# Sums of weight blocks made in DRAM by adding DMAs in place of VectorE additions

## The chip, the cores and the metric

The kernel runs on one core of a Trainium2 chip. The core has TensorE (PE; PEld is its weight load), VectorE (DVE), ScalarE (ACT) and GpSimd (POOL). DMAs are started from the queues of SyncE (SP), ACT and POOL and moved by 16 DMA engines. The metric is device time of one execution in microseconds, the median of several runs; a profile is of one execution.

## What is computed

The reference is a trunk of two layers on 512 tokens of width 1024, all in float32. Both layers widen to 2048.

```python
h = x                                               # (1, 512, 1024)
# layer 0: pooling mixer
u = rms_norm(h) @ pool_w_in                         # 1024 -> 4096
v, gate = split(u, 2)
p = multiscale_pool(v)                              # 4 groups of 512, windows 2, 4, 8, 16
m = einsum('btgc,gcd->btgd', p, w_grp) * scale
h = h + (m * silu(gate)) @ pool_w_out               # 2048 -> 1024
# layer 1: HGRN2, 16 heads of 128, chunks
q, fz, i, gate = split(rms_norm(h) @ hgrn_w_in, 4)  # 1024 -> 8192
o = hgrn2_chunk_scan(q, k(fz), i, cumsum(log_f(fz)))
h = h + (rms_norm_heads(o) * silu(gate)) @ hgrn_w_out
return rms_norm(h)
```

## The kernel before

**Products.** Each product of float32 operands is made of three matmuls of halves: an operand x is cut into hi (x rounded, made by ScalarE at L97) and lo (x minus hi, made by VectorE at L98), and `mm3` (L128 to L131) adds hi·hi, hi·lo and lo·hi in PSUM. Weights come in blocks of 128 x 2 x 512 floats, 512 KB, into the tiles wraw (three buffers), and are cut into whi and wlo (six buffers each); `piece` (L100) does one block: a load on SP's queue, then the cut. PE works through such products nearly all the time.

**Layer 0.** `l0` starts with eight blocks of x (h) and eight half blocks of w0i, 256 KB each, then four loads of x in the other layout (xt, 512 KB) for the norm. The norm factor rn_l is made of the sums ss in two steps: VectorE computes ms (L253), POOL takes the power (L255). PE spreads it over the partitions by L197 (`spread`), ScalarE copies the spread factor to rb (L203), and rb is used by every later step of the layer. In PE's instruction list L197 stands before the seventh of the eight steps of the first gates' projection. Then four groups g follow: `values`, `pool`, `project_out` of the group before, `gates0`, `mixed`.

**Layer 1.** The groups run through `group`: values of the group (`inputs`), attention, gates, output projection of the group before. The values of the last two groups are made together by `inputs2` (L457), when g is 2. It multiplies a 2 x 2 block matrix (two halves of the tokens, two groups) with seven block products in place of eight. Four of the seven use sums of weight blocks. With W(row, col) a quarter of 512 x 512 floats, two wraw blocks, they are

- W5 = W(0,0) + W(0,1), then W6 = W5 + W(1,1), then W4 = W6 + W(1,0): one chain, kept in the tiles named chain;
- W7 = W(0,1) + W(1,1), made in place in wraw.

Each sum is made on VectorE by `add` (L477 to L480, the instruction is L479), from blocks loaded by `load` (L474), and then cut like any other weight block. The other operand of four products is a sum of token blocks, which layer 1 has written to DRAM earlier (sums_fac) and reads back by `again` (tiles s, L454).

**What sets the order.** The program is written with tiles; a scheduler orders the instructions of each engine by priority, dependences and free buffers when the kernel is built, and `tc.high_priority(AHEAD)` moves loads and cuts ahead. At run time each engine takes its list strictly in order, and an instruction that waits for a semaphore holds up what stands behind it. POOL has no DMAs in this kernel.

Of the kernel before, what the change touches and what calls it, by code (L numbers as in the profile page):

```python
# [32 lines left out]
F32 = mybir.dt.float32  # L33
# [22 lines left out]
AHEAD0 = 85  # L56
AHEAD = 300
FLOOR = 1e-26
LEVELS = (1, 2, 4, 8, 16, 32, 64)


# [5 lines left out]
def trunk(ctx: ExitStack, tc: tile.TileContext, xT, x_d, par, ident_d, causal_d, mask_d, fg_d, w0_in, w0_grp, w0_out, w1_in, w1_out, out):  # L67
# [155 lines left out]
            nc.vector.tensor_tensor(out=h[n], in0=acc, in1=h[n], op=ALU.add)  # L223


    with tc.tile_pool(name="l0", bufs=1) as l0:
        xs, pieces = [], []
        wv = w0_in.rearrange("(k p) n -> p k n", p=P)
# [34 lines left out]
        def values(g):  # L263
            vs = []
            wv = None if g == 0 else load_in(w0_in, g * GC)
            for n in range(GT):
                acc = accs[n] if g == 0 else project(wv, n, xs)
                v = l0.tile([P, 16 + T], F32, name="v", tag="v", bufs=4)
                nc.gpsimd.memset(v[:, 0:16], 0.0)
                nc.vector.tensor_tensor(out=v[:, 16:], in0=acc, in1=rb, op=ALU.mult)  # L270
                vs.append(v)
            return vs

        def pool(g, vs):
            w, out = WINDOWS[g], []
            for n in range(GT):
                cur, step = vs[n], 1
                while step < w:
                    nxt = l0.tile([P, 16 + T], F32, name="win", tag="win", bufs=2)
                    if 2 * step < w:  # L280
                        nc.gpsimd.memset(nxt[:, 0:16], 0.0)
                    nc.vector.tensor_tensor(out=nxt[:, 16:], in0=cur[:, 16:], in1=cur[:, 16 - step:16 + T - step], op=ALU.add)
                    cur, step = nxt, 2 * step
                nc.vector.tensor_tensor(out=cur[:, 16:16 + w], in0=cur[:, 16:16 + w], in1=pp[:, cnts[g]:cnts[g] + w], op=ALU.mult)
                p = small.tile([P, T], F32, name="p", tag="hg", bufs=2)
                nc.vector.scalar_tensor_tensor(out=p, in0=cur[:, 16:], scalar=1.0 / w, in1=vs[n][:, 16:], op0=ALU.mult, op1=ALU.subtract)
                out.append(halves(p, "p", 4, l0))
            return out

        def gates0(g):  # L290
            wg = wg0 if g == 0 else load_in(w0_in, DI + g * GC)
            out = []
            for n in range(GT):
                acc = gates[n] if g == 0 and n < 2 else project(wg, n, xs)
                gt = l0.tile([P, T], F32, name="gt", tag="gt", bufs=2)
                nc.vector.tensor_tensor(out=gt, in0=acc, in1=rb, op=ALU.mult)
                sg = l0.tile([P, T], F32, name="sg", tag="sg", bufs=2)
                nc.scalar.activation(out=sg, in_=gt, func=AF.Sigmoid)  # L298
                gs = l0.tile([P, T], F32, name="gs", tag="gs", bufs=4)
                nc.gpsimd.tensor_tensor(out=gs, in0=gt, in1=sg, op=ALU.mult)  # L300
                out.append(gs)
            return out

        def mixed(g, ps_, gates):
            wm = load_in(w0_grp[g])
            out = []
            for n in range(GT):
                acc = project(wm, n, ps_)
                z = small.tile([P, T], F32, name="z", tag="hg", bufs=2)
                c = C_PS + g * GT + n  # L310
                nc.vector.scalar_tensor_tensor(out=z, in0=acc, scalar=pp[:, c:c + 1], in1=gates[n], op0=ALU.mult, op1=ALU.mult)
                out.append(halves(z, "z", 8, l0))
            return out

        zprev = None
        for g in range(NG):
            vs = values(g)
            px = pool(g, vs)
            if zprev is not None and g < NG - 1:
                project_out(load_out(w0_out, g - 1), zprev)  # L320
            gts = gates0(g)
            z = mixed(g, px, gts)
            if g == NG - 1:
                project_out(load_out(w0_out, g - 1), zprev)
            zprev = z
# [24 lines left out]
    def hgrn(ctx, general, h):  # L350
# [107 lines left out]
        def inputs2(g):  # L458

            w = w1_in.rearrange("(k p) n -> p k n", p=P)

            def block(row, col, i):
                c = 2 * DI + (g + col) * GC
                return w[:, 4 * row + 2 * i:4 * row + 2 * i + 2, c:c + GC]

            def load(*a):
                raw = wpool.tile([P, 2, GC], F32, name="wraw", tag="wraw", bufs=RAW)
                with tc.high_priority(AHEAD):
                    nc.sync.dma_start(out=raw, in_=block(*a))  # L474
                return raw

            def add(out, x, y):  # L477
                with tc.high_priority(AHEAD):
                    nc.vector.tensor_tensor(out=out, in0=x, in1=y, op=ALU.add)  # L479
                return out  # L480

            def cut(x):
                hi = wpool.tile([P, 2, GC], F32R, name="whi", tag="whi", bufs=WB)
                lo = wpool.tile([P, 2, GC], F32R, name="wlo", tag="wlo", bufs=WB)
                with tc.high_priority(AHEAD):
                    split(x, hi, lo)
                return [(hi[:, 0], lo[:, 0]), (hi[:, 1], lo[:, 1])]

            def product(accs, x, pieces):
                for b, acc in enumerate(accs):  # L490
                    t = slice(b * P, (b + 1) * P)
                    for k, ((xh, xl), (wh, wl)) in enumerate(zip(x, pieces)):
                        mm3(acc, xh[:, t], xl[:, t], wh, wl, k == 0, k == 3)

            two = lambda: [ps.tile([P, T], F32, name="mm", tag="mm", bufs=4) for _ in range(2)]
            v = l1.tile([P, TB, GC], F32, name="vn", tag="vn", bufs=1)
            v1 = [l1.tile([P, GC], F32, name="v1", tag="gs", bufs=4) for _ in range(TB)]
            chain = []
            s = again

            def plus(out, acc, x):
                nc.vector.tensor_tensor(out=out, in0=acc, in1=x, op=ALU.add)  # L502

            def times(x, by, t):
                nc.scalar.activation(out=x, in_=x, func=AF.Copy, scale=by[:, t:t + 1])

            a = two()
            product(a, own[0], cut(load(0, 0, 0)) + cut(load(0, 0, 1)))
            for b in range(2):
                nc.scalar.copy(out=v[:, 2 + b], in_=a[b])  # L510
            a = two()
            product(a, own[1], cut(load(1, 0, 0)) + cut(load(1, 0, 1)))
            for b in range(2):
                plus(v[:, b], a[b], v[:, 2 + b])
                times(v[:, b], rn, b)
            pieces = []
            for i in range(2):
                x, y = load(0, 0, i), load(0, 1, i)
                chain.append(l1.tile([P, 2, GC], F32, name="chain", tag="f", bufs=2))
                pieces += cut(add(chain[i], x, y))  # L520
            c = two()
            product(c, s(0), pieces)
            s2 = s(1)
            pieces = [x for i in range(2) for x in cut(add(chain[i], chain[i], load(1, 1, i)))]
            a = two()
            product(a, s2, pieces)
            s3 = s(2)
            for b in range(2):
                plus(v1[b], a[b], v[:, 2 + b])
            pieces = []  # L530
            for i in range(2):
                x, y = load(0, 1, i), load(1, 1, i)
                pieces += cut(add(x, x, y))
            a = two()
            product(a, s3, pieces)
            s4 = s(3)
            for b in range(2):
                plus(v[:, 2 + b], a[b], v1[b])
                plus(v1[2 + b], c[b], v[:, 2 + b])
                plus(v1[b], c[b], v1[b])  # L540
                times(v1[2 + b], nrn, 2 + b)
                nc.scalar.dma_start(out=v_d[2 + b], in_=v1[2 + b])
            pieces = [x for i in range(2) for x in cut(add(chain[i], chain[i], load(1, 0, i)))]
            a = two()
            product(a, own[3], pieces)
            for b in range(2):
                plus(v[:, 2 + b], a[b], v[:, 2 + b])
                times(v[:, 2 + b], rn, 2 + b)
            a = two()
            product(a, s4, cut(load(1, 1, 0)) + cut(load(1, 1, 1)))  # L550
            for b in range(2):
                plus(v1[b], a[b], v1[b])
                times(v1[b], nrn, b)
                nc.scalar.dma_start(out=v_d[b], in_=v1[b])
            return v
# [411 lines left out]
```

## Time and profile before

| | us |
|---|---|
| median of 3 runs (lowest to highest) | 840.53 (840.23 to 841.55) |
| the profiled execution | 840.38 |
| its span, first to last instruction | 838.6 |
| PE busy in the span | 816.0 |
| VectorE busy | 582.5 |
| ScalarE busy | 295.1 |
| POOL busy | 151.4 |

The profiled execution takes 1.8 us more than its span. Busy time of PE is the union of its matmuls, which overlap: a matmul of 512 columns is listed with 0.39 us, but one starts every 0.23 us. The rows below are from this execution; "idle before" names what ended the idle time of an engine.

### The profile page before, as it was taken

To read this page: it belongs to the slowest core of one execution; us is meant where nothing else is said; L and a number is where in the kernel's file an instruction comes from. 1 tells how busy PE (TensorE), PEld (TensorE's weight loads), DVE (VectorE), ACT (ScalarE), POOL (GpSimd) and SP (SyncE) were. 2 spreads that over 40 slices of the span, in tenths; PEclk is the share of its full clock that TensorE was granted. 3 is DMA by queue.
4 is the path that set the end of the run, shared out by engine and by line. 5 is a ranking of instruction groups with operands and counts; after the bars stand their busy time and mean duration, and the time that the engine had idled before them with its cause. 6 is when DMAs were issued, how large, how long until landed. Compare 5 with 4: busy or idle time off the path is not lost.

```text
span 838.6 us, 10334 instructions
## 1 busy us (share of the span) xinstructions
PE 816.0 (97%) x3878; PEld 682.0 (81%) x3878; DVE 582.5 (69%) x889; ACT 295.1 (35%) x500; POOL 151.4 (18%) x198
## 2 busy tenths in 40 slices
PE   9999999999999999998999999999988999998995
PEld 8888888888888888887888788888767888887984
DVE  5787546844777463997489973279988545995764
ACT  7542133323235153415442242332236134223222
POOL 0020010002011041440134300305300031332200
PEclk9999999999999999999999999999999999999999
DMA  9532234323134155034733231233387243321202
GB/s 347 185 102 75 77 100 151 101 78 117 57 101 130 62 175 163 26 101 152 250 101 100 93 110 36 66 101 100 101 269 259 74 152 101 101 75 55 73 1 104
DMA packets 48299, 96.89 MB, mean 116 GB/s; under 512 B 3696, under 2 KB 8048, under 8 KB 48240
## 3 DMA queue, kind: packets, MB, share of 16 engines
q1 hardware_dynamic: 42336, 85.99, 31.4%
q10 hardware_dynamic: 5904, 10.15, 3.3%
q8 instruction: 32, 0.52, 0.2%
q14 instruction: 27, 0.22, 0.1%
HBM read 86.69 MB, written 9.44 MB: 115 GB/s over the span
## 4 chain that ended last, share of the span: by engine, by line
PE 76%; DVE 16%; DMA 3%; issue 2%; ACT 2%; POOL 0%; POOLq 0%; DVEq 0%; ACTq 0%
PE mm L130 23%; PE mm L129 23%; PE mm L131 22%; DVE r L720 4%; DVE wlo L98 4%; DMA wraw<-in_w1i 3%; PE a L775 2%; PE a L777 1%; PE a L753 1%; ACT whi L97 1%; DVE f L705 1%; DVE q L724 1%; DVE f L706 1%; PE a L736 1%; DMA wraw<-in_w1o 1%
## 5 line engine op out<-in xcount | busy, mean ns | idle before, releaser
L129 PE MATMUL mm<-xh,whi 128*128 128x512 f32 x624 | 244.3, 391 | 0.0
L131 PE MATMUL mm<-xh,wlo 128*128 128x512 f32 x624 | 243.0, 390 | 0.0
L130 PE MATMUL mm<-xl,whi 128*128 128x512 f32 x624 | 243.0, 389 | 0.0
L97 ACT CAST whi<-wraw 128x1024 fp32r<-128x1024 f32 (+1 forms) x140 | 141.5, 1025 | 226.5 <-PE mm L130 108.3
L98 DVE TENSOR_TENSOR wlo<-wraw,whi 128x1024 fp32r<-128x1024 f32 (+1 forms) x140 | 172.7, 1258 | 49.7 <-ACT whi L97 47.9
L131 PEld LDWEIGHTS mm<-xh,wlo 128*128 128x128 f32 x624 | 117.1, 188 | 24.7 <-DVE wlo L98 0.2
L129 PEld LDWEIGHTS mm<-xh,whi 128*128 128x128 f32 x624 | 117.2, 188 | 24.2 <-DVE h L223 0.3
L130 PEld LDWEIGHTS mm<-xl,whi 128*128 128x128 f32 x624 | 117.2, 188 | 23.8
L720 DVE RECIPROCAL r<-r 128x512 f32<-128x512 f32 x16 | 53.4, 3338 | 0.0
L131 PE MATMUL mm<-zh,wlo 128*128 128x512 f32 x128 | 49.8, 389 | 0.0
L129 PE MATMUL mm<-zh,whi 128*128 128x512 f32 x128 | 49.8, 389 | 0.0
L130 PE MATMUL mm<-zl,whi 128*128 128x512 f32 x128 | 49.8, 389 | 0.0
L223 DVE TENSOR_TENSOR h<-mm,h 128x512 f32<-128x512 f32 x32 | 21.9, 688 | 28.5 <-PE mm L131 28.1
L380 DVE TENSOR_TENSOR ht<-mm,ht 128x512 f32<-128x512 f32 x32 | 22.0, 687 | 27.9 <-PE mm L131 27.9
L129 PE MATMUL mm<-whi,z1h 128*128 128x512 f32 x96 | 37.9, 395 | 0.0
L300 POOL TENSOR_TENSOR gs<-gt,sg 128x512 f32<-128x512 f32 x16 | 21.9, 1372 | 87.9 <-ACT sg L298 87.9
L131 PE MATMUL mm<-whi,z1l 128*128 128x512 f32 x96 | 37.4, 390 | 0.0
L582 POOL TENSOR_TENSOR gs<-fz,s 128x512 f32<-128x512 f32 x16 | 22.4, 1402 | 83.3 <-ACT s L580 83.2
L130 PE MATMUL mm<-wlo,z1h 128*128 128x512 f32 x96 | 37.4, 389 | 0.0
L594 POOL TENSOR_TENSOR ro<-mo,mhalf 128x4 f32<-128x4 f32 x16 | 16.2, 1014 | 113.1 <-DVE mo L592 113.1
L130 PE MATMUL mm<-wlo,xh 128*128 128x512 f32 x88 | 34.6, 393 | 1.0 <-DVE wlo L98 1.0
L129 PE MATMUL mm<-whi,xh 128*128 128x512 f32 x88 | 34.7, 394 | 0.7 <-DVE v L502 0.7
(179 smaller groups left out, 1271.1 us busy)
## 6 DMA issues: line engine op xcount, KB each, us to landing
wraw<-in_w1i SPq DMA_DIRECT2D x74, 512.0 KB, 4.0
wraw<-in_w0i SPq DMA_DIRECT2D x28, 512.0 KB, 4.5
wraw<-in_w0o SPq DMA_DIRECT2D x16, 512.0 KB, 4.1
wraw<-in_w1o SPq DMA_DIRECT2D x16, 512.0 KB, 4.1
wraw<-in_w0g SPq DMA_DIRECT2D x8, 512.0 KB, 3.8
s<-sums_fac SPq DMA_DIRECT2D x16, 256.0 KB, 4.4
h<-in_xT SPq DMA_DIRECT2D x8, 256.0 KB, 5.3
wraw<-in_w0i SPq DMA_DIRECT2D x8, 256.0 KB, 5.3
```

The costliest lines, as they stand in the source:

```text
L97: nc.scalar.copy(out=hi, in_=src)
L98: nc.vector.tensor_tensor(out=lo, in0=src, in1=hi, op=ALU.subtract)
L129: nc.tensor.matmul(out, lh, rh, start=start, stop=False)
L130: nc.tensor.matmul(out, lh, rl, start=False, stop=False)
L131: nc.tensor.matmul(out, ll, rh, start=False, stop=stop)
L223: nc.vector.tensor_tensor(out=h[n], in0=acc, in1=h[n], op=ALU.add)
L300: nc.gpsimd.tensor_tensor(out=gs, in0=gt, in1=sg, op=ALU.mult)
L380: nc.vector.tensor_tensor(out=ht[b][:, c], in0=acc, in1=ht[b][:, c], op=ALU.add)
L582: nc.gpsimd.tensor_tensor(out=gs, in0=gt, in1=sg, op=ALU.mult)
L594: nc.gpsimd.tensor_tensor(out=ro[:, :, 0], in0=mo, in1=mhalf[:, :TB], op=ALU.pow)
L720: nc.vector.reciprocal(out=r, in_=r)
L775: nc.tensor.matmul(o[:, b], Ads[pr][:, j, t], v[:, b, n * P:(n + 1) * P], start=True, stop=b == 0)
```

## The change

The four sums of the third group are made in DRAM. A DRAM tensor wsum holds W5, W6, W7 and W4. A new function `weight_sums(step)` is called twice in each of groups 1, 2 and 3 of layer 0, in six steps: copy W(0,0) and W(0,1), add W(0,1) and W(1,1) to them, copy W5 to W6, add W(1,1), copy W6 to W4, add W(1,0). Each step is done in halves of 256 rows (512 KB), so there are 16 DMAs on POOL's queue, eight copies and eight with `accum_op=ALU.add`. `inputs2` then loads each sum as two blocks by `piece`, and `load`, `add`, `cut` and the tiles chain are gone from it. The setting dynamic_dma_scratch_size of the build goes from 512 to 1024.

```diff
+PAIRS = (2,)
+    wsum = {g: dram.tile([4, 4 * P, GC], F32, name=f"wsum{g}") for g in PAIRS}
+
+    def quarter(g, row, col):
+        c = 2 * DI + (g + col) * GC
+        return w1_in[row * 4 * P:(row + 1) * 4 * P, c:c + GC]
+
+    def weight_sums(step):
+
+        for g in PAIRS:
+            w5, w6, w7, w4 = (wsum[g][i] for i in range(4))
+            todo = (((w5, quarter(g, 0, 0), False), (w7, quarter(g, 0, 1), False)),
+                    ((w5, quarter(g, 0, 1), True), (w7, quarter(g, 1, 1), True)),
+                    ((w6, w5, False),), ((w6, quarter(g, 1, 1), True),),
+                    ((w4, w6, False),), ((w4, quarter(g, 1, 0), True),))[step]
+            for out_, in_, adding in todo:
+                for r in range(0, 4 * P, 2 * P):
+                    if adding:
+                        nc.gpsimd.dma_start(out=out_[r:r + 2 * P], in_=in_[r:r + 2 * P], accum_op=ALU.add)
+                    else:
+                        nc.gpsimd.dma_start(out=out_[r:r + 2 * P], in_=in_[r:r + 2 * P])
...
             vs = values(g)
+            if g:
+                weight_sums(2 * g - 2)
             px = pool(g, vs)
...
             gts = gates0(g)
+            if g:
+                weight_sums(2 * g - 1)
             z = mixed(g, px, gts)
...
-            pieces = []
-            for i in range(2):
-                x, y = load(0, 0, i), load(0, 1, i)
-                chain.append(l1.tile([P, 2, GC], F32, name="chain", tag="f", bufs=2))
-                pieces += cut(add(chain[i], x, y))
             c = two()
-            product(c, s(0), pieces)
+            product(c, s(0), pieces(wsum[g][0]))
             s2 = s(1)
-            pieces = [x for i in range(2) for x in cut(add(chain[i], chain[i], load(1, 1, i)))]
             a = two()
-            product(a, s2, pieces)
+            product(a, s2, pieces(wsum[g][1]))
...
-    nc = bacc.Bacc("TRN2", target_bir_lowering=False, num_devices=1, dynamic_dma_scratch_size=512)
+    nc = bacc.Bacc("TRN2", target_bir_lowering=False, num_devices=1, dynamic_dma_scratch_size=1024)
```

How the instruction lists change is shown at three places. First POOL at the start of layer 0, before:

```order
L94 MEMSET mhalf 128x8
L269 MEMSET v 128x16 x4
L255 ISA
L255 TENSOR_TENSOR rn_l_327<-ms,mhalf 128x4
L269 MEMSET v 128x16 x2
```

and now, each row with the semaphores that it waits for (DMASW0 to DMASW7 are counted up by POOL's own DMAs; the digits are their lanes):

```order
L292 MEMSET v 128x16 x4
L246 DMA wsum_104<-in_w1i 256x512 x4
L244 DMA wsum_104<-in_w1i 256x512 [waits DMASW0_49]
...
L244 DMA wsum_104<-in_w1i 256x512 [waits DMASW3_49]
L246 DMA wsum_104<-wsum_104 16x8192 [waits DMASW4_49]
...
L244 DMA wsum_104<-in_w1i 256x512 [waits DMASW1_49]
L246 DMA wsum_104<-wsum_104 16x8192 [waits DMASW2_49]
...
L244 DMA wsum_104<-in_w1i 256x512 [waits DMASW7_49,DMASW5_49]
L278 ISA
L278 TENSOR_TENSOR rn_l_328<-ms,mhalf 128x4 [waits DVE_49,Pool_49]
```

All 16 DMAs stand between the four memsets and rn_l (L246 are the copies, L244 the adds; L278 is what was L255), not in groups 1 to 3; 12 of them wait for an earlier one. PE's list is the same there.

Second VectorE at the beginning of `inputs2`, before (L608 and z1l belong to the gating of the group before, L72x to the preparation of this one):

```order
L720 RECIPROCAL r<-r 128x512
L479 TENSOR_TENSOR chain<-wraw 128x1024
L724 TENSOR_TENSOR q<-q,r 128x4x64
L725 TENSOR_TENSOR q<-q,f 128x4x64
L608 SCALAR_TENSOR_TENSOR z_4914<-a,pp,gs 128x512
L98 TENSOR_TENSOR wlo<-chain,whi 128x1024
L98 TENSOR_TENSOR z1l<-z_4914,z1h 128x512
L608 SCALAR_TENSOR_TENSOR z_4925<-a,pp,gs 128x512
L479 TENSOR_TENSOR chain<-wraw 128x1024
```

and now:

```order
L718 RECIPROCAL r<-r 128x512
L99 TENSOR_TENSOR wlo<-wraw,whi 128x1024 x3
L722 TENSOR_TENSOR q<-q,r 128x4x64
L723 TENSOR_TENSOR q<-q,f 128x4x64
L606 SCALAR_TENSOR_TENSOR z_4931<-a,pp,gs 128x512
L606 SCALAR_TENSOR_TENSOR z_4942<-a,pp,gs 128x512
L511 TENSOR_TENSOR vn<-mm,vn 128x512
```

Cuts of three blocks stand where one addition stood, ahead of the rest of the preparation.

Third SP's queue in `inputs2` and just behind it, before (L474 are its weight loads, L454 the loads of s, w1o the output weights):

```order
L106 DMA wraw<-in_w1i 128x2x512 x12
L474 DMA wraw<-in_w1i 128x2x512 x13
L454 DMA s<-sums_fac 128x2x256 x3
L474 DMA wraw<-in_w1i 128x2x512
L454 DMA s<-sums_fac 128x2x256 x2
L474 DMA wraw<-in_w1i 128x2x512 x2
L454 DMA s<-sums_fac 128x2x256
L474 DMA wraw<-in_w1i 128x2x512 x2
L106 DMA wraw<-in_w1o 128x1024
L454 DMA s<-sums_fac 128x2x256 x2
L106 DMA wraw<-in_w1o 128x1024 x3
```

and now:

```order
L107 DMA wraw<-in_w1i 128x2x512 x16
L107 DMA wraw<-wsum_104 128x2x512 x8
L481 DMA s<-sums_fac 128x2x256
L107 DMA wraw<-in_w1i 128x2x512
L481 DMA s<-sums_fac 128x2x256
L107 DMA wraw<-in_w1i 128x2x512
L107 DMA wraw<-in_w1o 128x1024
L481 DMA s<-sums_fac 128x2x256 x2
L107 DMA wraw<-in_w1o 128x1024 x2
L481 DMA s<-sums_fac 128x2x256 x4
L107 DMA wraw<-in_w1o 128x1024
```

The last 18 loads of weights for `inputs2` become 14, and the second eight loads of s stand behind all eight of wsum.

## Rows read from the trace of the kernel before

**Rows 1.** The page, part 1: busy us, share of span, instructions.

```profile
PE 816.0 (97%) x3878; PEld 682.0 (81%) x3878; DVE 582.5 (69%) x889; ACT 295.1 (35%) x500; POOL 151.4 (18%) x198
```

**Rows 2.** Stretches in the stage of `inputs2`: the first row names the columns.

```profile
core 0: us, PE busy (x) PEld busy (x) DVE busy (x) ACT busy (x) POOL busy (x), PEclk, DMA share, GB/s
600.00:660.00 60.00, 52.84 (x257) 42.67 (x256) 51.86 (x76) 24.82 (x30) 1.74 (x3) 1.00 0.72 234
...
620.00:630.00 10.00, 8.85 (x52) 7.36 (x50) 7.29 (x8) 3.42 (x4) 0.00 (x0) 1.00 0.91 298
```

**Rows 3.** Line L479: duration ns min/median/max, first and last start; then who waited.

```profile
L479 DVE TENSOR_TENSOR chain<-chain,wraw x4: 1208/1222/1227, 609.0 to 627.7; 128x1024 f32<-128x1024 f32 x4
L479 DVE TENSOR_TENSOR chain<-wraw x2: 1153/1178/1204, 601.9 to 607.3; 128x1024 f32<-128x1024 f32 x2
L479 DVE TENSOR_TENSOR wraw<-wraw x2: 1215/1220/1225, 616.5 to 622.5; 128x1024 f32<-128x1024 f32 x2
...
ACT whi L97: 15.2, 8
```

**Rows 4.** Chain of waits in `inputs2`: start us, us, what.

```profile
607.25 1.22 DVE chain L479
...
608.49 3.94 DMA wraw<-in_w1i
...
612.51 1.23 DVE chain L479
```

**Rows 5.** Waits from 553 to 700 us: waiter, releaser, us, times, longest.

```profile
PE mm L129 <- ACT whi L97: 2.8, 2, 1.6
...
PE mm L130 <- DVE wlo L98: 1.6, 2, 1.4
...
PE a L753 <- DVE Ad L739: 1.0, 1, 1.0
```

**Rows 6.** POOL in order of time at the start: start us, us, instruction.

```profile
0.90 0.24 POOL L269 MEMSET v<- 128x16 f32 x4
21.70 1.01 POOL L255 TENSOR_TENSOR rn_l<-ms,mhalf 128x4 f32<-128x4 f32 x1 [20.56 <-DVE ms L253]
```

**Rows 7.** PE in order of time, the spreading of the norm factor.

```profile
31.51 1.05 PE L197 MATMUL a<-ident,rn_l 128*128 128x128 f32 x8
```

**Rows 8.** Stretches of the first 30 us; columns as in rows 2.

```profile
0.00:5.00 5.00, 4.02 (x19) 4.03 (x20) 0.26 (x1) 2.42 (x4) 0.61 (x10) 1.00 0.63 199
5.00:10.00 5.00, 5.00 (x23) 3.96 (x23) 3.86 (x6) 3.79 (x7) 0.00 (x0) 1.00 1.02 368
10.00:15.00 5.00, 5.00 (x24) 4.14 (x23) 4.99 (x9) 4.79 (x8) 0.00 (x0) 1.00 1.04 391
15.00:20.00 5.00, 5.00 (x24) 4.14 (x23) 1.75 (x3) 4.25 (x8) 0.00 (x0) 1.00 1.02 414
20.00:25.00 5.00, 5.00 (x24) 4.14 (x23) 1.40 (x2) 3.27 (x5) 1.01 (x1) 1.00 0.64 233
25.00:30.00 5.00, 5.00 (x24) 4.14 (x23) 3.67 (x3) 2.16 (x3) 0.00 (x0) 1.00 0.72 233
```

**Rows 9.** DMA issues: line, queue, count, KB each, median us to landing.

```profile
wraw<-in_w1i SPq DMA_DIRECT2D x74, 512.0 KB, 4.0
wraw<-in_w0i SPq DMA_DIRECT2D x28, 512.0 KB, 4.5
...
h<-in_xT SPq DMA_DIRECT2D x8, 256.0 KB, 5.3
wraw<-in_w0i SPq DMA_DIRECT2D x8, 256.0 KB, 5.3
xt<-in_x SPq DMA_DIRECT2D x4, 512.0 KB, 6.7
```

**Rows 10.** Chain that ended last, PE's first pieces: start us, us, what.

```profile
0.98 4.64 PE a L86 x20
...
31.67 0.89 PE a L197 x8
```

More of the change, by code (lines that the diff above doesn't have):

```diff
@@ L458, in inputs2, with pieces, product @@
         def inputs2(g):
[L465 to L479, printed above, removed]
-                return out
[L482 to L489, printed above, removed]
+            def pieces(src):
+                v = src.rearrange("(k p) n -> p k n", p=P)
+                out = []
+                for i in range(0, 4, 2):
+                    hi, lo = piece(v[:, i:i + 2])
+                    out += [(hi[:, 0], lo[:, 0]), (hi[:, 1], lo[:, 1])]
+                return out
+            def product(accs, x, w):
                 for b, acc in enumerate(accs):
                     t = slice(b * P, (b + 1) * P)
-                    for k, ((xh, xl), (wh, wl)) in enumerate(zip(x, pieces)):
+                    for k, ((xh, xl), (wh, wl)) in enumerate(zip(x, w)):
                         mm3(acc, xh[:, t], xl[:, t], wh, wl, k == 0, k == 3)
@@ L497, in inputs2 @@
             v1 = [l1.tile([P, GC], F32, name="v1", tag="gs", bufs=4) for _ in range(TB)]
-            chain = []
             s = again
@@ L507, in inputs2 @@
             a = two()
-            product(a, own[0], cut(load(0, 0, 0)) + cut(load(0, 0, 1)))
+            product(a, own[0], pieces(quarter(g, 0, 0)))
             for b in range(2):
@@ L511, in inputs2 @@
             a = two()
-            product(a, own[1], cut(load(1, 0, 0)) + cut(load(1, 0, 1)))
+            product(a, own[1], pieces(quarter(g, 1, 0)))
             for b in range(2):
@@ L529, in inputs2 @@
                 plus(v1[b], a[b], v[:, 2 + b])
[L530 to L533, printed above, removed]
             a = two()
-            product(a, s3, pieces)
+            product(a, s3, pieces(wsum[g][2]))
             s4 = s(3)
@@ L542, in inputs2 @@
                 nc.scalar.dma_start(out=v_d[2 + b], in_=v1[2 + b])
-            pieces = [x for i in range(2) for x in cut(add(chain[i], chain[i], load(1, 0, i)))]
             a = two()
-            product(a, own[3], pieces)
+            product(a, own[3], pieces(wsum[g][3]))
             for b in range(2):
@@ L549, in inputs2 @@
             a = two()
-            product(a, s4, cut(load(1, 1, 0)) + cut(load(1, 1, 1)))
+            product(a, s4, pieces(quarter(g, 1, 1)))
             for b in range(2):
```

## The prediction

> **What bounds the kernel now.** First the page: PE is busy for 816.0 us of the span of 838.6 [rows 1]. So the time is PE's work plus the 22.6 us in which PE stands, and an edit to another engine or to a queue counts only where it makes PE stand or lets it go on. Two places matter, and the code names them: the stage that the change relieves (`inputs2`, layer 1, third group) and the start, where the order of the change puts its new DMAs.
>
> The stretches by stage come next [rows 2]. From 600 to 660 us PE is busy for 52.84 us of 60: it stands for 7.16 us, a third of all that it loses in the kernel. The DMA engines are at 0.91 there between 620 and 630. The lines of that stage say why [rows 3]: eight VectorE additions at L479, 1.18 to 1.22 us each, sum the weight blocks, and ScalarE, which cuts the result, waited 15.2 us for them. The chain of waits [rows 4] shows the pattern: a load of wraw, then an addition, then the next load. The waits of PE [rows 5] that come from there are 2.8 us on ScalarE's whi and 1.6 us on VectorE's wlo; 1.0 us on the causal copy (Ad) has another cause.
>
> The start is read last. POOL clears four borders by 1.14 us, does nothing for 20.56 us, and computes the norm factor rn_l at 21.70 us, in 1.01 us [rows 6]. PE uses it in L197 at 31.51 us [rows 7], so rn_l has about 8.8 us to spare. L197 stands in the middle of a projection, and PE takes its instructions in order: whatever delays rn_l past 31.5 us stops PE. In the same stretch the DMA engines are full, 1.02 to 1.04 of their time at 368 to 414 GB/s from 5 to 20 us [rows 8].
>
> **The change part by part.** Removed from layer 1: the eight additions (2 x 1.178 + 4 x 1.222 + 2 x 1.220 = 9.7 us of VectorE) and four of 18 weight loads, 0.52 MB each, since a sum is now read as one block. VectorE's order there becomes plain cuts. I take back the 7.16 us that PE stands less what waits for something else (the 1.0 us above and about as much on ScalarE's kt and other pieces, some 1.7 us): 5.5 us. The bounds are 0, if the loads of s, now later on SP behind the eight wsum loads, take the place of the additions, and 7.16. I stay near the upper end: 14 weight loads and eight of s are 9.4 MB for some 45 us, 210 GB/s, while the engines showed up to 414 [rows 8]; and s is reloaded two products before it is needed.
>
> Added: 16 DMAs on POOL's queue, 0.52 MB each, eight copies and eight adds. By the text they belong to groups 1 to 3 of layer 0. The order shows all 16 in one piece directly behind the four memsets and ahead of rn_l, nearly each with a wait for an earlier one. So POOL, which stood idle for 20.56 us at no cost, now stands in a chain: four copies, four adds, two copies, two adds, two copies, then the issue of the last two adds; only then rn_l. Behind it on POOL stand rn_l, the borders of v and the gates' products; for rn_l waits PE itself. Nothing hides that beyond the 8.8 us.
>
> No row shows a DMA from POOL, a copy from DRAM to DRAM, or an add. I bound them by bytes. A copy moves one block; an add needs both operands, the sum so far and the addend, so I count two blocks, 1.05 MB (lower bound one block). Ahead of rn_l 14 DMAs must have landed: 8 copies and 6 adds, 4.19 + 6.29 = 10.5 MB. SP's loads moved 9.2 MB in the first 30 us: the six stretches are (199 + 368 + 391 + 414 + 233 + 233) x 5 us [rows 8]. Together 19.7 MB; at 390 GB/s, the middle of the full stretches, 50.5 us. The chain begins at 1.2 us, so the bytes are through at 51.7. Latency comes on top where the chain is alone: a 512 KB load lands after 4.0 us [rows 9], of which 0.524 MB at 390 GB/s are 1.3, so 2.7 us for each hand-over from one DMA to the next that waits on it. The first three hand-overs lie beside SP's traffic or the second pair; the last two do not: 5.4 us. POOL is free at 57.1, rn_l is done at 58.1, and L197 starts at about 58.2 instead of 31.5: PE stands for 26.7 us more. SP's loads slow down as well (xt took 6.7 us when the engines were full [rows 9], and would take longer), but PE has until 58 us for what they feed; that delay lies inside the stall.
>
> On the price of an add the Trainium skill (Collectives: The Full Stack, The bandwidth ceiling: the fold count and why AG ≠ RS ≠ AR) says that a reducing transfer is about half as fast as a copy because it needs two source reads, not because of the addition itself. No run here shows it yet; by that rule the sum stays as above, and at a copy's price it would be 8 us less.
>
> After the stall PE may start slowly. The twenty matmuls of L86 at the very start, with nothing before them, take 4.64 us, 0.232 each; eight of L197 of the same size take 0.89, 0.111 each [rows 10]; the granted clock reads 1.00 in both stretches [rows 8], so the rows give the loss and not its cause. If PE comes back like that, twenty such pieces cost 2.4 us. I take it in full; the other end is 0.
>
> Sum against the profiled execution, 840.4 us: + 26.7 + 2.4 - 5.5 = 864.0. The median of the runs is 840.5, 0.15 us above it, so the forecast is **864 us**.
>
> **The rivals.**
>
> The DMAs of POOL do not compete with SP's loads. A copy inside DRAM might run beside loads to the chip at a rate of its own. Then the chain is 10.5 MB at 390 GB/s, 26.9 us, from 1.2 us on, plus 5.4 of hand-overs: POOL is free at 33.5, L197 starts at 34.7, the stall is 3.2 us, and with 5.5 gained the time is 838, slightly faster. It decides at a stall of 5.5 us. For it: nothing in the rows excludes it. Against it: the engines are at 1.02 to 1.04 with SP's loads alone [rows 8]. The Trainium skill (DMA: Bandwidth & Descriptors, Issuing engines are not separate DMA queues) speaks against it too: DMAs from SP, ACT and GpSimd end on the same sixteen engines and interleave. By that rule this rival falls and the 864 stands; the trace, full with one queue, agrees as far as it goes.
>
> Adds at a copy's price and no gaps. What PE needs ahead of L197 is 7.9 MB (eight h and eight w0i of 256 KB, four xt and three w0i of 512 KB [rows 9]), and 14 blocks are 7.3 MB: 15.2 MB at 414 GB/s, 36.7 us. POOL is free at 37.9, the stall is 7.5 us, and with no slow start and the whole 7.2 us gained the time is 840.7: no change. That is the lowest end with shared engines; with hand-overs of 5.4 us and a gain of 5.5 it is 848.
>
> Adds in series, each alone. If one add must land before the next is issued and each takes two landings of 4.0 us, six adds are 48 us; the four copies at half of 390 GB/s are 10.8 + 2.7 us, the next pair 6.7, the last copy 4.0. POOL is free at 73.4, the stall is 43 us, and the time is 880. With the landing of a full stretch, 6.7 us, for each block of an add, the adds are 80 us: POOL is free near 105 and the time is about 913. For it: every add waits for an earlier DMA, and the queue is new to this kernel.
>
> The change doing nothing in layer 1 (the s loads late) takes the 5.5 away: 869, inside the range.
>
> **How the numbers follow.** Shared engines with dear adds, 850 to 890: 0.60. Cheap adds, 843 to 850: 0.12. Adds in series at 890 and above: 0.17, half of it over 905. Own rate, 834 to 838.5: 0.06. About level, 838.8 to 842.2: 0.05. The range 843 to 905 leaves out the two last ones and the far tail, about 0.2. A measurement of this kernel tells about 0.2% (1.7 us) from no change: faster 0.06, same 0.05, slower 0.89.
>
> **What would show it.** Right: the wait of rn_l on POOL ends near 57 us, PE has one gap of 20 to 30 us ahead of L197 (L198 in the new text), the DMA share of the first 50 us is near 1, and between 600 and 660 us (shifted by the stall) PE stands for under 2.5 us with no L479. Wrong: rn_l done before 31.5 us (no stall, faster by 5), or PE's gap elsewhere. If the gap is right and the stage at 600 us still loses 7 us, the gain was the wrong term; if the gap is 10 or 60 us, the price of an add was.

## The result and the profile after

The changed kernel takes 879.3 us, median of four runs (876.3 to 881.5), against 840.5 before: ratio 1.046, 95% interval 1.042 to 1.050. It is slower, by the mechanism that the prediction put first, but by 39 us and not by 24. The profiled execution took 877.3 us, with a span of 875.3.

The waits of PE come first, as in [rows 5]: waiter, releaser, us in total, times, longest.

```profile
PE a L198 <- POOL rn_l L278: 31.0, 1, 31.0
...
PE mm L130 <- DVE vn L511: 1.5, 1, 1.5
PE mm L130 <- DMA s<-sums_fac: 1.4, 1, 1.4
```

One wait of 31.0 us holds most of the loss. L198 is L197 of before. It starts at 71.47 us, where [rows 7] had 31.51. PE in order of time (start us, us, instruction, idle before):

```profile
40.05 0.39 PE L132 MATMUL a<-xh,wlo 128*128 128x512 f32 x1
71.47 2.08 PE L198 MATMUL a<-ident,rn_l 128*128 128x128 f32 x8 [31.03 <-POOL rn_l L278]
73.20 0.77 PE L130 MATMUL a<-xh,whi 128*128 128x512 f32 x1
```

POOL in order of time, to be read beside [rows 6]: L246 are the copies, L244 the adds, L278 the pow that makes rn_l.

```profile
1.43 1.98 POOL L246 DMA_DIRECT2D wsum<-in_w1i  x3 [0.28 <-issue]
8.86 0.57 POOL L246 DMA_DIRECT2D wsum<-in_w1i  x1 [5.44 <-issue]
12.99 0.96 POOL L244 DMA_DIRECT2D wsum<-in_w1i  x1 [3.56 <-issue]
22.20 0.91 POOL L244 DMA_DIRECT2D wsum<-in_w1i  x1 [8.26 <-issue]
32.30 0.88 POOL L244 DMA_DIRECT2D wsum<-in_w1i  x1 [9.18 <-issue]
38.36 0.90 POOL L244 DMA_DIRECT2D wsum<-in_w1i  x1 [5.18 <-issue]
38.92 1.36 POOL L246 DMA_DIRECT2D wsum<-wsum  x2
47.38 0.91 POOL L244 DMA_DIRECT2D wsum<-in_w1i  x1 [7.10 <-DMA wsum<-wsum]
53.50 0.91 POOL L244 DMA_DIRECT2D wsum<-in_w1i  x1 [5.21 <-issue]
...
69.33 0.91 POOL L244 DMA_DIRECT2D wsum<-in_w1i  x1 [7.43 <-issue]
70.02 1.40 POOL L278 TENSOR_TENSOR rn_l<-ms,mhalf 128x4 f32<-128x4 f32 x1
```

An issue takes under 1 us. Between two issues POOL stands, and for six of the eight adds the cause is given as "issue": nothing that the profile shows held it. Those six stands add up to 38.8 us. The stretches of the start (columns as in [rows 2]) show that the DMA engines were not what was short at the end:

```profile
40.00:50.00 10.00, 0.44 (x2) 0.02 (x1) 2.45 (x2) 1.63 (x2) 1.19 (x2) 0.79 1.03 330
50.00:60.00 10.00, 0.00 (x0) 0.00 (x0) 0.00 (x0) 0.00 (x0) 1.73 (x3) 0.50 0.73 150
60.00:70.00 10.00, 0.00 (x0) 0.00 (x0) 0.00 (x0) 0.00 (x0) 1.78 (x3) 0.50 0.49 105
70.00:80.00 10.00, 8.53 (x31) 7.24 (x32) 5.55 (x10) 2.81 (x3) 1.42 (x2) 0.68 0.46 105
```

While PE stands, its granted clock falls to 0.50 (1.2 of 2.4 GHz), and it stays there for the first 5.0 us after the stand: the eight matmuls of L198 take 2.08 us instead of 1.05. The 0.68 of the last row is a mean of two parts:

```profile
71.47:76.50 5.03, 5.03 (x16) 4.35 (x17) 2.05 (x3) 2.81 (x3) 0.00 (x0) 0.50 0.58 102
76.50:80.00 3.50, 3.50 (x17) 2.89 (x16) 3.50 (x8) 0.00 (x0) 0.00 (x0) 1.00 0.45 150
```

The relieved stage, 36 us later than in [rows 2]:

```profile
636.00:696.00 60.00, 55.80 (x276) 45.94 (x275) 49.50 (x74) 24.27 (x31) 3.17 (x2) 1.00 0.63 210
```

PE stands for 4.2 us there, where [rows 2] had 7.16; the eight additions of [rows 3] are gone. What is left are the waits for vn and for the loads of s shown above. The DMA view (queue, packets, MB, share of the span on 16 engines; issues with KB each and median us to landing, as in [rows 9]):

```profile
q0 software_dynamic: 2880, 8.39, 4.1%
...
wsum<-in_w1i POOLq DMA_DIRECT2D x12, 512.0 KB, 7.0
...
h<-in_xT SPq DMA_DIRECT2D x8, 256.0 KB, 9.1
...
xt<-in_x SPq DMA_DIRECT2D x4, 512.0 KB, 9.8
```

q0 is POOL's queue, new in this kernel. SP's start loads landed later than in [rows 9]: h after 9.1 us instead of 5.3, xt after 9.8 instead of 6.7.

One table for what follows. "First product" is the start of the norm factor's matmuls (L197, L198), "late mark" the start of the last transposes ahead of the relieved stage, "rest" the span less that mark. All come from the profiled executions.

| kernel | first product | late mark | rest | time of that run |
|---|---|---|---|---|
| before | 31.51 | 592.47 | 246.1 | 840.4 |
| after | 71.47 | 634.57 | 240.7 | 877.3 |
| e1_ring1216 | 58.19 | 621.37 | 241.2 | 864.5 |
| e2_copies | 46.97 | 608.36 | 241.5 | 851.7 |
| e3_late | 31.45 | 629.56 | 242.1 | 873.5 |
| e4_nosums | 31.60 | 592.58 | 243.2 | 837.7 |
| e5_sumsonly | 73.93 | 637.44 | 247.6 | 886.8 |
| e6_spread | 31.93 | 595.44 | 241.2 | 838.5 |
| e7_start4 | 33.27 | 596.64 | 242.1 | 840.7 |
| e8_spread1216 | 31.38 | 592.12 | 241.3 | 835.3 |
| e9_halfadds | 61.90 | 624.67 | 243.3 | 869.8 |

So the change is two separate things: +42.1 us by the late mark, -5.4 behind it.

### The profile page after: what moved, and what is told of

The parts are those of the page before. It is cut to its first block, busy times and chain, and to the rows that moved or that the text cites. A ratio compares the mean times of both kernels' runs of the same rounds, so it can differ in the third digit from the quotient of the medians.

```text
span 875.3 us, 10353 instructions
## 1 busy us (share of the span) xinstructions
PE 820.3 (94%) x3878; PEld 683.9 (78%) x3878; DVE 574.3 (66%) x881; ACT 294.4 (34%) x500; POOL 163.5 (19%) x214
## 3 DMA queue, kind: packets, MB, share of 16 engines
q0 software_dynamic: 2880, 8.39, 4.1%
HBM read 92.99 MB, written 17.83 MB: 127 GB/s over the span
## 4 chain that ended last, share of the span: by engine, by line
PE 74%; DVE 11%; issue 7%; DMA 4%; POOL 1%; ACT 1%; POOLq 0%; DVEq 0%; SPq 0%; ACTq 0%
PE mm L131 22%; PE mm L130 22%; PE mm L132 22%; DVE r L718 3%; DVE wlo L99 3%; PE a L773 2%; DMA wsum<-wsum 1%; PE a L751 1%; PE a L775 1%; DMA wraw<-wsum 1%; DMA wraw<-in_w1i 1%; PE a L734 1%; ACT whi L98 1%; DMA s<-sums_fac 1%; DVE q L722 1%
## 5 line engine op out<-in xcount | busy, mean ns | idle before, releaser
L98 ACT CAST whi<-wraw 128x1024 fp32r<-128x1024 f32 (+1 forms) x146 | 147.7, 1025 | 239.6 <-PE mm L131 111.8
L99 DVE TENSOR_TENSOR wlo<-wraw,whi 128x1024 fp32r<-128x1024 f32 (+1 forms) x146 | 180.2, 1258 | 52.9 <-ACT whi L98 51.0
L130 PEld LDWEIGHTS mm<-xh,whi 128*128 128x128 f32 x624 | 117.5, 188 | 26.7 <-ACT whi L98 2.6
L293 DVE TENSOR_TENSOR v<-mm,rb 128x512 f32<-128x512 f32 x16 | 10.8, 687 | 38.5 <-ACT rb L204 30.8
```

The lines of the kernel that those rows point to most:

```text
L98: nc.scalar.copy(out=hi, in_=src)
L99: nc.vector.tensor_tensor(out=lo, in0=src, in1=hi, op=ALU.subtract)
L130: nc.tensor.matmul(out, lh, rh, start=start, stop=False)
```

## The experiments

e4, e6 and e8 were run several times. The others were run once, and only differences of several us are read from their times. On their chips the kernel before took 839.2 us (e1, e2, e4, e5), 840.6 (e3, e6, e7, e8) and 841.6 (e9).

### The two halves apart

e5 is the kernel before with the sixteen DMAs added at the place where the change puts them. e4 is the changed kernel without them; inputs2 reads four single quarters in place of the sums:

```diff
-            if g:
-                weight_sums(2 * g - 2)
...
-            product(c, s(0), pieces(wsum[g][0]))
+            product(c, s(0), pieces(quarter(g, 0, 0)))
```

> The kernel before with the 16 DMAs of the change added (the sums are made in DRAM and not read); layer 1 still adds on VectorE. This is the loss at the start by itself. Theory A, the loss lies wholly at the start: about 42 us, so 882 (878 to 888), with the norm factor at about 71 us and the stage at 600 us of before, shifted, unchanged. Rival: part of the loss came with the new loads of layer 1: under 875.

> The changed kernel without any DMA for sums in layer 0; layer 1 loads single weight blocks where it would load sums (14 loads, no additions; the sums are left out of the computation). This is the gain in layer 1 by itself. Theory A, layer 1 gains what the two traces show between the transposes ahead of the stage and the end (+42.1 us there, +36.7 us at the end): 5.4 us, so 835.1 (834.4 to 836). Rival: the smaller delay at the end comes from somewhere else, and the time is 839 to 841.

e5 took 886.8 us, with its first product at 73.93: the loss is whole without any change in layer 1. e4 took 836.47 (835.17 to 837.65), ratio 0.996, interval 0.9947 to 0.9972: the gain alone, 2.7 us by the medians and 3.4 by the ratio, was less than the 5.4 of the table. Its profiled execution lost part of it to the clock. Two stretches of e4's stage:

```profile
610.00:620.00 10.00, 7.53 (x26) 5.71 (x26) 7.72 (x9) 5.62 (x7) 0.00 (x0) 0.83 0.87 259
620.00:630.00 10.00, 8.10 (x31) 6.26 (x30) 5.31 (x7) 3.10 (x4) 0.00 (x0) 0.83 0.90 310
```

and the same two of e8 (below), which does the same products there:

```profile
610.00:620.00 10.00, 7.43 (x33) 5.37 (x31) 8.17 (x10) 6.17 (x7) 0.00 (x0) 1.00 0.83 255
620.00:630.00 10.00, 8.09 (x34) 6.38 (x35) 6.44 (x9) 2.81 (x4) 0.00 (x0) 1.00 0.96 321
```

PE stands equally long in both, but in e4 the granted clock is 0.83 in the mean of each stretch: for a part of each it was at the lower level, 0.50. By that row 3.4 us of full-speed work were not done (0.17 x 20).

### What an add costs: room, bytes, or place

Three small edits. e1 gives POOL's DMAs more room for their descriptors; e2 makes the adds plain copies; e9 cuts each add in two of 128 rows, with the room of 1024 as in the change.

```diff
-    nc = bacc.Bacc("TRN2", target_bir_lowering=False, num_devices=1, dynamic_dma_scratch_size=1024)
+    nc = bacc.Bacc("TRN2", target_bir_lowering=False, num_devices=1, dynamic_dma_scratch_size=1216)
```

```diff
-                        nc.gpsimd.dma_start(out=out_[r:r + 2 * P], in_=in_[r:r + 2 * P], accum_op=ALU.add)
+                        nc.gpsimd.dma_start(out=out_[r:r + 2 * P], in_=in_[r:r + 2 * P])
```

```diff
-                        nc.gpsimd.dma_start(out=out_[r:r + 2 * P], in_=in_[r:r + 2 * P], accum_op=ALU.add)
+                        for u in (r, r + P):
+                            nc.gpsimd.dma_start(out=out_[u:u + P], in_=in_[u:u + P], accum_op=ALU.add)
```

> The changed kernel with dynamic_dma_scratch_size 1216 in place of 1024, nothing else. In the changed kernel POOL stood 38.8 us in six waits ahead of adds that the profile cannot name, and each of these adds was issued just when the add before it had landed. Theory A, the room kept for POOL's DMAs holds one add at a time: a little more room lets a second add in, most of the unnamed waits go, the last part of the chain (from 47 us on, where the DMA engines are at 0.73 and 0.49) gets shorter by 5 to 11 us, and the profiled time falls from 877 to 866 to 872. Theory B, the waits are the adds' own time: nothing moves, 875 to 880.

> The changed kernel with the eight adds made plain copies of the same blocks (no sums are formed). The order of POOL stays the same. Theory A, an add costs about two blocks of the DMA engines' time and goes alone: with copies the chain ends near 53 us instead of 70, the first use of the norm factor on PE comes near 54 instead of 71.5, and the time is near 860. Theory B, an add costs no more than a copy and the chain is set by its hand-overs from one DMA to the next: the time stays within 3 us of 877.

> The changed kernel with every add cut in two of 128 rows (16 adds of 256 KB in place of 8 of 512 KB); same bytes, same ring of 1024, same place ahead of the pow. Theory R (an add of 256 rows leaves no room in the ring for the next one, so that the 512 KB adds ran one at a time): two halves fit and overlap as in the run with the larger ring; last DMA issued near 57 us, first product at 56 to 62 us, time 863 to 869. Rival L (each add costs a latency of its own on POOL's queue, whatever its size): eight more adds cost 5 us each at the least, first product at 100 us or later, time above 900. Rival B (only the bytes count, whatever the room): nothing changes, 875 to 882.

**e1** took 864.5 us, 12.8 below the changed kernel's profiled run, 11.8 below its fastest, and 1.5 below the range that the theory of the room gave. POOL in order of time:

```profile
1.43 2.54 POOL L246 DMA_DIRECT2D wsum<-in_w1i  x4 [0.28 <-issue]
...
39.46 0.93 POOL L244 DMA_DIRECT2D wsum<-in_w1i  x1 [11.99 <-DMA wsum<-wsum]
40.74 0.90 POOL L244 DMA_DIRECT2D wsum<-in_w1i  x1 [0.35 <-DMA wsum<-wsum]
...
56.74 1.39 POOL L278 TENSOR_TENSOR rn_l<-ms,mhalf 128x4 f32<-128x4 f32 x1
```

All four copies now go out at once, where the fourth had waited 5.44 us, and two adds go out 1.3 us apart. The unnamed stands ahead of the adds fall from 38.8 us to 18.8 (7.67, 2.82, 5.29 and 3.05, ahead of the first four adds); they do not go altogether. Between 50 and 60 us the DMA engines are at 0.94, where the changed kernel had 0.73:

```profile
50.00:60.00 10.00, 2.15 (x11) 1.81 (x9) 2.45 (x2) 2.09 (x2) 3.53 (x4) 0.62 0.94 263
```

**e9** took 869.8 us, 0.8 above the range given for the room, 5 us below the rival of the bytes and far below that of a price for each add: the room of 1024 takes halves several at a time.

```profile
38.02 2.54 POOL L245 DMA_DIRECT2D wsum<-in_w1i  x3 [8.66 <-DMA wsum<-wsum]
```

The same bytes, in the same place, in more pieces, end 9.5 us earlier (the pow at 60.48 us). So neither bytes nor a fixed price for each add explains those 10 to 13 us; the room does. The rows fit one count: a room of 1024 takes three copies or three half adds but one whole add, and a room of 1216 takes four copies or two adds. A whole add takes the room of about two copies.

The packets of POOL's queue say the same. In e6 (below) one add stands alone from 130.0 to 138.1 us, and four copies of weight blocks from 47 to 61 us (packets, MB, share of the stretch):

```profile
q0 software_dynamic: 272, 0.52, 47.0%
```

```profile
q0 software_dynamic: 576, 2.10, 43.1%
```

An add is 272 packets, such a copy 144. Half an add is 144 too, for e9 has 128 packets more than the changed kernel (3008 and 2880). Three of these are 432, two adds 544, four copies 576: a room of 1024 that ends between 432 and 544 packets, and one of 1216 that holds 576, fit all the rows. That the room is counted in this way is inferred from the fit.

The changed kernel itself shows what ends a stand. The add issued at 22.20 us lands 9.8 us later, at 32.0, and the next is issued at 32.30:

```profile
wsum<-in_w1i POOLq DMA_DIRECT2D x1, 512.0 KB, 9.8
```

The other four unnamed stands that have an add ahead of them end 0.3 us after its landing too. By the code the second to fourth add need only the copies of `step` 0, the last of which was issued at 8.86 us and landed 7.0 us later.

**e2** took 851.7 us, first product at 46.97: 8 us below the 860 of the theory that adds are dear, and far below the rival's 877. It takes away the price of the adds and their room at once, so it does not tell the two apart; e1 and e9 do. Its adds do not add, so its POOL queue can be priced beside the other:

```profile
q0 software_dynamic: 1856, 8.39, 2.6%
```

Sixteen copies are 2.6% of 849.9 us on all sixteen engines: 22.1 us, 1.4 each. In the changed kernel the sixteen DMAs are 4.1% of 875.3 us: 35.9 us in 2880 packets. Less eight copies, an add is 3.1 us, 2.2 times a copy, and its packets are 1.9 times those of a copied weight block. The price moves with what runs beside: the same sixteen DMAs take 33.6 us in e1 (3.9% of 862.6) and 39.3 in e6 (4.7% of 836.6), which by the same working would make an add 2.8 to 3.5 us. The bytes row shows none of it (8.39 MB in both). The Trainium skill (Collectives: The Full Stack, The bandwidth ceiling: the fold count and why AG ≠ RS ≠ AR) gives 1.93 for a reduction between cores against a copy and puts it down to two read descriptors for each chunk. The 2.2 and 1.9 here agree with the ratio; that an add reads twice shows in no row, for the profile's HBM read is 92.99 MB with and without adding. The Trainium skill (DMA: Bandwidth & Descriptors, SWDGE vs HWDGE vs iDMA) also says that DMAs from GpSimd have their descriptors written into rings in SBUF. That POOL stands when its room is used up is what e1 and e9 show.

Nor would free adds have saved the start. In e2 PE stands for weights, not for the pow:

```profile
PE a L130 <- ACT whi L98: 5.9, 1, 5.9
PE mm L130 <- ACT whi L98: 3.7, 4, 1.7
```

### Another place

Behind which instruction of POOL the DMAs are issued was set by hand. `behind` holds the pow, and for e6 to e8 also the borders of the values and the gates' products (gs), so that each step stands where the text of the change writes it.

```diff
-            for out_, in_, adding in todo:
...
+            with tc.issue_after(behind[-1].ins):
+                for out_, in_, adding in todo:
...
-            nc.gpsimd.tensor_tensor(out=rn, in0=ms, in1=mhalf[:, :TB], op=ALU.pow)
+            behind.append(nc.gpsimd.tensor_tensor(out=rn, in0=ms, in1=mhalf[:, :TB], op=ALU.pow))
```

e3 puts all sixteen right behind the pow. e6 spreads them over layer 0. e7 is e6 with the first four copies left at the very start. e8 is e6 with the room of 1216.

> All sixteen DMAs stand on POOL right behind the pow (rn_l) instead of ahead of it; nothing else is changed. Theory A (the loss is one of place: what stands behind the DMAs on POOL waits for the whole chain, which holds POOL for some 60 us): the first product starts at 31.5 us as before the change, but the first products gs of the gates (41 to 55 us in the kernel before) stand behind the chain now and come at 80 to 90 us; PE stands some 20 us in front of layer 0's first mixing, time 848 to 865. Theory B (the loss is the DMA engines' share that the start loads have to give up): with the start loads gone by 21.7 us, nothing is left to lose, time 834 to 838.

> The same sixteen DMAs, spread over layer 0: the first four behind the last borders of group 1's values, four adds and two copies behind group 1's gates, two adds and two copies behind group 2's, the last two adds behind group 3's. Theory A: POOL has nothing urgent there and the start loads are done; the start is as before (first product at 31.5 us), the gain in layer 1 stays, 833.5 to 837 (gain 2.5 to 5.5 against 839 to 840.5). Theory B' (the adds cost wherever they lie, by POOL's standing or by the weight loads beside them): one or two stands of 3 to 9 us in layer 0, 840 to 850.

> As the spread kernel, but the first four copies (2 MB read, 2 MB written) are left at the very start, ahead of the pow. It prices the competition with the start loads alone. Theory A' (the start loads lose what the copies take): the loads that the first product waits for come up to 5.5 us later; first product at 34 to 37 us, time 837 to 842. Rival (the loads lose nothing that the norm does not hide): first product at 31.5, time as the spread kernel's.

> The spread kernel with room for two adds in POOL's ring (1216 instead of 1024). Theory A: POOL's standing is off the path there, so the same time as the spread kernel within 1 us. Theory B': POOL's stands are shorter, so 2 to 6 us below the spread kernel.

**e3** took 873.5 us, above both expectations: that a loss of place would follow was right, 20 us for it was too little. The first product is in time at 31.45, and the chain now holds up the next thing on POOL, the gates' products. POOL, then who waited (between 45 and 90 us), then PE:

```profile
82.97 2.82 POOL L326 TENSOR_TENSOR gs<-gt,sg 128x512 f32<-128x512 f32 x2
```

```profile
DVE gt L322 <- POOL gs L326: 37.2, 1, 37.2
```

```profile
86.40 0.79 PE L131 MATMUL mm<-pl,whi 128*128 128x512 f32 x1 [33.03 <-DVE pl L99]
```

VectorE stands for gs, the split of the mixed values (pl) stands behind that on VectorE, and PE stands 33.0 us for it. SP's start loads were gone by then, so their bytes are not the reason.

**e7**: 840.7 us, pow at 26.99 against 21.56 in e6. Four copies at the start (2.1 MB read and written) delay the loads behind the pow by 5.4 us, as its first theory had it, but the slack of [rows 6] hides the late pow: the first product, at 33.27, is below the 34 to 37 given and 1.3 us behind e6, of which 0.7 us are waits for weight cuts and none a wait for the pow.

**e6** took 838.44 us (835.26 to 844.32), ratio 0.9981, interval 0.9961 to 1.0001: no clear gain, and between the two theories (833.5 to 837, 840 to 850). The start is clean. POOL and PE in order of time, and what VectorE waited for from 130 to 192 us:

```profile
138.17 0.91 POOL L247 DMA_DIRECT2D wsum<-in_w1i  x1 [7.00 <-issue]
146.68 0.88 POOL L247 DMA_DIRECT2D wsum<-in_w1i  x1 [7.60 <-issue]
```

```profile
DVE win L310 <- POOL v L295: 5.1, 1, 5.1
```

```profile
163.08 0.50 PE L132 MATMUL mm<-zh,wlo 128*128 128x512 f32 x1 [1.77 <-DVE wlo L99]
```

Four adds one at a time hold POOL for 24 us, a border behind them comes late, VectorE stands 5.1 us for it and PE 1.8. So the rival of e6's expectation, POOL's standing, was right in kind and smaller than its price. That the spread of e6's runs comes from there too is argued from this one profile, not shown.

**e8** took 835.64 us (835.32 to 836.05), ratio 0.9939, interval 0.9923 to 0.9955: 2.8 below e6, as its theory of shorter stands had it (2 to 6), 5.0 below the kernel before and far below the changed one. PE has no wait from 130 to 192 us. POOL there:

```profile
129.65 1.89 POOL L247 DMA_DIRECT2D wsum<-in_w1i  x2
138.83 0.90 POOL L247 DMA_DIRECT2D wsum<-in_w1i  x1 [7.28 <-issue]
141.37 0.88 POOL L247 DMA_DIRECT2D wsum<-in_w1i  x1 [1.64 <-issue]
```

## Why the prediction was right, point by point

**The place of the loss** was right: POOL stands in the chain, the pow comes last, PE stands at the norm factor's matmuls. e5 shows that it comes from the DMAs alone, and e3, e6 and e8 that it is the order on POOL: with the same sixteen DMAs the first product is at 31.4 to 31.9 us.

**The size of the stall** was the mis-sized term: 26.7 us forecast, 40.0 measured (71.47 less 31.51). The failing step is "POOL is free at 57.1": it was free at 70.0. Its bytes, 19.7 MB at 390 GB/s with an add as two blocks, are consistent with e1, where POOL was free at 56.7 and the engines stayed nearly full; and an add costs the engines 2.2 copies (e2). What failed is that only the last two hand-overs would leave the engines idle. With room for one add, nearly every add stands alone: share 0.73 from 50 to 60 us and 0.49 after that. In the runs, room for a second add is worth 13.3 us at the first product (71.47 to 58.19), as much as the whole error.

**The start loads** are slowed, inside the stall, as said. PE came to L198 at 40.4 us instead of 31.5, which costs nothing while the pow comes at 70.0. In e2, where PE no longer waits for the pow, its first product is still 15 us late.

**The slow return** was right: 2.4 forecast, 2.1 measured (late mark +42.1 less +40.0). The cause left open there is now on rows: a granted clock of 0.50 while PE stood and for 5.0 us of work behind the stand, of which it costs half, 2.5 us.

**The gain in layer 1** came out as forecast, 5.5 against 5.4, but by luck and not by its own working. PE's stand in the stage fell from 7.16 to 4.2 us, which is 3.0 and not 5.5: new waits for vn and s, 1.5 and 1.4 us, took part of it. The prediction also put too little down to other causes, 1.7 us: the waits for cuts in [rows 5] are 4.4 of the 7.16, so 2.7 were not the additions'. The sign named in advance, a stand of under 2.5 us, did not come. A further 1.6 us are the clock. In before its mean is 0.92 over 20 us late in the layer (0.08 x 20); in after, at the same place of the program 37 us later, it is 1.00. The stretches of PE alone (busy us, clock, DMA share, GB/s), of before and then of after:

```profile
760.00:780.00 20.00, 19.66 (x104) 0.92 0.29 100
```

```profile
797.00:817.00 20.00, 18.87 (x106) 1.00 0.30 102
```

The last 0.8 us I did not trace. Nine profiles with the new layer 1 give 2.8 to 5.4 us of gain by the table's column "rest", and e5, which keeps the old layer 1, has 247.6 there: the clock moves both sides. An estimate without it takes off half of the time that the granted clock was 0.50 between the late mark and the last 20 us: 1.7 us in before, e3 and e9, 3.4 in e4 and e5, nothing in the other six. The old layer 1 then has 244.4 (before) and 244.2 (e5), the new one 239.8 to 242.1, with 241.2 in the middle. So the edit gives some 3 us, as PE's stands say; by the times of several runs it is 2.7 (e4) to 5.0 (e8). The 5.5 was more than any of these.

**The rivals.** A rate of its own for POOL's DMAs falls: four copies alone delay the pow by 5.4 us (e7), and sixteen delay PE's weights (e2). Adds at a copy's price would have been 851.7 (e2), above the 840.7 to 848 given, because PE stands for weights there. No gain in layer 1 falls by the table. Adds in series, each alone, with 880 us and a chain end of 73.4, came nearest: 879.3 us and 70.0. It was the better model of the chain, though for another reason than the one given for it. The adds did not stand alone because each waits for an earlier DMA; six of the eight stood for room, and more room (e1) or smaller pieces (e9) let them overlap. That 879.3 lies inside the range is luck in part: the sum gave 864, and the 850 to 890 that was written for it also holds the 880 of this rival.

## What to carry to other kernels

A DMA on an engine's queue is also an instruction of that engine. Before work is handed to an idle engine's queue, look at what stands behind it there, and whether an engine that works all the time waits for that. The same sixteen DMAs cost 47.6 us ahead of the pow (e5 against 839.2) and left the late mark where it was in quiet stretches with room for two adds (e8: 592.12 against 592.47); there with room for one it came 3.0 us late (e6). An adding DMA takes about two copies of engine time and of descriptor room: give it room for two, or cut it, before judging it.

## What the runs showed of the hardware

- A DMA that adds in DRAM (256 rows of 2 KB) takes 272 packets (e6) and 3.1 us of all sixteen engines, a copy of the same block 144 and 1.4 (e6, e2); the profile's bytes and its HBM read are the same for both.
- When the room for descriptors is used up, POOL stands in the issue, 3.6 to 9.2 us a time in the changed kernel, and the profile names no releaser ("issue"). Six such stands made 38.8 us; five of them end 0.3 us after the add ahead has landed.
- After PE's stand of 31 us the granted clock was 0.50 (1.2 GHz) for another 5.0 us of matmuls, then 1.00. After stands of 4 to 5 us in two pieces it was 0.83 in the mean of 20 us in one profile (e4) and 1.00 in others of the same products (e6, e8). What decides between these two is open.
